# A four-layer decoder step on one core: the last k tile of a stage's first block is held back, the MLP's mean square is spread over the next blocks, and gate blocks go ahead of the first chain

## The chip, the cores and the metric

The kernel runs on one NeuronCore of a Trainium2 chip. The metric is the device time of the whole program in microseconds (us), the median of several runs. The trace comes from one profiled execution, with its own time. Engines: PE is TensorE (matmuls), DVE is VectorE, ACT is ScalarE, POOL is GpSimd, SP issues the weight transfers.

## The reference

One step of a decoder trunk of four layers for 288 tokens (256 of a prompt, 8 x 4 of samples), model width 1024. A layer is a token mixer and an MLP, each behind an RMS norm and added to x. The mixers are retention (layer 0), SSD (1), gated DeltaNet (2) and retention (3).

```
def _rms(x, w):  return x * lax.rsqrt(jnp.mean(x * x, axis=-1, keepdims=True) + 1e-6) * w
def _sqrelu_mlp(h, w_up, w_down):  return jnp.square(jax.nn.relu(h @ w_up)) @ w_down   # 1024 -> 4096 -> 1024
for i in range(4):
    out, s = (_retention, _ssd, _gdn)[i % 3](_rms(x, norm_mix[i]), ...)   # @ w_in, conv, scan, gate, norm, @ w_out
    x = x + out
    x = x + _sqrelu_mlp(_rms(x, norm_mlp[i]), mlp_w_up[i], mlp_w_down[i])
y = _rms(x, norm_final)
```

The outputs are y for prompt and samples and the new states of the mixers. SSD and gated DeltaNet (gdn) have a causal convolution over four positions and, per token, small gates: a step size or decay `la` (SSD), `g` and `beta` (gdn), from 32 columns of the input projection.

## The kernel before, in words

Tokens lie along the free axis (288 columns), channels on the 128 partitions. x is eight tiles of 128 x 288, one per k tile.

`dense` multiplies by a weight matrix, 128 output columns (a block) at a time. The weights come in as float32, 256 columns (two blocks, 1 MB) in a transfer, and are split for the matmul: ACT copies a half of a block's k tiles (four, 128 x 512) to a rounded `wh` (L212), DVE subtracts to get the rest `wl` (L215). There are four buffers for these halves: two blocks' worth. A block is 8 k tiles of three matmuls each, `xh·wh` (L227), `xl·wh` (L228), `xh·wl` (L229), where `xh` and `xl` are the activations split in the same way (`ah` and `al` in the second half of the MLP). A block gathers in a PSUM tile `psd` and is evacuated by a callback right behind its 24 matmuls.

The activations of a stage come out of the stage before, tile by tile: `norm_add(k)` scales x by the norm's gain and splits it to `xh` (ACT, L302) and `xl` (DVE, L303), and adds x's square to `acc` (DVE for the last tile, L298). The division by the root mean square is not waited for: the first matmuls run on unscaled x, and a factor `rb` is multiplied in behind. `tok_rstd` sums `acc` over the partitions on PE (`ps_st`, L330), DVE adds the constant (`ms`, L333), POOL takes the power (`rs_y`, L268); `bcast` spreads the result over the partitions on PE (`ps_bc`, L342), and ACT copies it to `rb` (L351). `norm_finish` is all of that.

With the eighth tile `norm_add` leaves a list `hold`: of the next six `wl` casts the first two (the first block) may go at once, the other four (the second and third block) are issued behind the eighth tile's `xl`.

An MLP runs `up` and `down` in four quarters q of 8 blocks each; behind the 8 blocks of `up` of q = 0 comes `norm_finish`. A mixer runs in four units m: the SSD and gdn layers start with `gates_tok` (one block of 32 columns, then `norm_finish`, then small transposes `ps_gt`), and the chain that turns the gates into decays (`ps_ct`, `cth`, `cts`). `units` runs the first projection and then weaves, for every m, the chain (scan) with gate blocks, further projections and output blocks. `conv_dense` evacuates a projection block to `U` (L815), keeps its last columns in `tl` (L818, transposed later on PE as `ps_cs`, L850) and does the convolution on DVE (L832).

What sets the order: a scheduler puts each engine's instructions in a row when the program is built, by the order in which the code emits them and by priorities; at run time every engine works through its own row, and waits where an operand isn't there.

Of the kernel before, what the change touches and what calls it, by code (L numbers as in the profile page):

```python
# [123 lines left out]
def run(gen):  # L124
    for _ in gen:
        pass


class K:
    def __init__(self, ctx, tc, I, O, C, layers):  # L130
        self.tc, self.nc, self.I, self.O, self.C = tc, tc.nc, I, O, C
        self.layers = layers
        self.hold, self.started = [], False
        self.ahead = 0
# [53 lines left out]
    def dense(self, xh, xl, w, evac, pre=None):  # L188
# [4 lines left out]
        for c0 in range(0, n, cw):  # L193
# [10 lines left out]
            for s0 in range(0, cn, sw):  # L204
# [13 lines left out]
                for o in range(0, sn, 128):  # L218
                    os = slice(o, min(o + 128, sn))
                    self.ahead -= 1  # L220
                    if 0 <= self.ahead < 2:
                        ps = self.ps("psd", "s")[:, 0:T]
                    else:
                        ps = self.psd.tile([128, T], F32, name="psd", tag="d")
                    po = ps[:os.stop - o]
                    for k in range(kt):
                        nc.tensor.matmul(po, lhsT=hs[k][:, os], rhs=xh[k], start=(k == 0), stop=False)  # L227
                        nc.tensor.matmul(po, lhsT=hs[k][:, os], rhs=xl[k], start=False, stop=False)  # L228
                        self.last_mm = nc.tensor.matmul(po, lhsT=ls[k][:, os], rhs=xh[k], start=False,  # L229
                                                        stop=(k == kt - 1))  # L230
                    evac((c0 + s0 + o) // 128, ps)
                    yield kt * 3 * 0.124

    def weave(self, chain, *fillers):
# [110 lines left out]

    def norm_finish(self):
        nc = self.nc
        r = self.tok_rstd([self.nx["acc"]], D)
# [100 lines left out]
    def mlp(self, mp, i, nxt, consts):  # L449
# [4 lines left out]
        late = self.later(mp) if self.later else iter(())  # L454
        self.later = None

        def blocks(gen):
            for _ in gen:
                next(late, None)

        for q in range(4):
            ah, al = self.act_tiles()
# [6 lines left out]
                nc.scalar.activation(ah[o], v, AF.Square)  # L469
                nc.vector.tensor_tensor(out=al[o], in0=a, in1=ah[o], op=ALU.subtract)  # L470

            blocks(self.dense(xh, xl, I["mlp_w_up"][i, :, q * 1024:(q + 1) * 1024], up))
            if q == 0:
                rb = self.norm_finish()
                rb2 = mp.tile([128, T], F32, name="rb2", bufs=1)
                nc.vector.tensor_tensor(out=rb2, in0=rb, in1=rb, op=ALU.mult)
# [30 lines left out]

        yield from self.dense(act[0], act[1], w[m * 512:(m + 1) * 512, :], ev)

    def units(self, proj, chain, gate, fin, w, i, side=None):  # L510
        acts = {}

        def finish(m):
# [3 lines left out]
        def out(n):  # L517
            yield from self.w_out(w, n, acts.pop(n), i)
# [419 lines left out]
    def ssd(self, ctx, j, i):  # L938
# [46 lines left out]
        def bcm(ap, n):  # L985
            return ap.unsqueeze(1).broadcast_to([ap.shape[0], n, ap.shape[1]])


        tok = self.gates_tok(rp, xh, xl, w[:, 6144:6176], wg, rb)
        V.tensor_tensor(out=tok, in0=tok, in1=bcm(dtb, 3), op=ALU.add)  # L990
        tok2 = tok.rearrange("p g h -> p (g h)")
# [44 lines left out]
        units = {}  # L1036

        def proj(m):
            xs = [rp.tile([128, T], F32, name="xs", tag=f"xs{a}", bufs=2) for a in range(4)]
            tails, tl = [], rp.tile([128, 8, 35], F32, name="tl", tag="tl", bufs=2)  # L1040
            Bt = [rp.tile([128, T], F32, name="Bt", tag=f"Bt{a}") for a in range(2)]
            Ct = [rp.tile([128, T], F32, name="Ct", tag=f"Ct{a}") for a in range(2)]
            for (c0, ch, dst) in ((4096 + m * 256, 16 + 2 * m, Bt), (5120 + m * 256, 24 + 2 * m, Ct),
                                  (2048 + m * 512, 4 * m, xs)):
                yield from self.conv_dense(rp, xh, xl, w[:, c0:c0 + len(dst) * 128], ch, rb, cw, cb, bias, dst, tails, tl)
            units[m] = {"xs": xs, "B": Bt, "C": Ct, "tails": tails}

        def scan(m):
            u = units[m]
# [193 lines left out]
        self.units(proj, scan, gate, fin, I["ssd_w_out"][j], i)  # L1243

# [4 lines left out]
    def gdn(self, ctx, j, i):  # L1249
# [54 lines left out]
        def small(name, *sh):  # L1304
            return rp.tile([128] + list(sh), F32, name=name)


        tok = self.gates_tok(rp, xh, xl, w[:, 6144:6176], wg, rb)
        beta, g = small("beta", 3, 16), small("g", 3, 16)
        ax = self.t128("ax")[:, 0:48].rearrange("p (g h) -> p g h", g=3)  # L1310
# [45 lines left out]
        units = {}  # L1356
# [6 lines left out]

        Z = rp.tile([128, 2, DB, 40], F32, name="Z")
        G.memset(Z, 0.0)

        def proj(m):
            qk = rp.tile([128, 4, T], F32, name="qk", tag="qk", bufs=2)
            v = [rp.tile([128, T], F32, name="v", tag=f"v{a}") for a in range(4)]
            tails, tl = [], rp.tile([128, 8, 35], F32, name="tl", tag="tl", bufs=2)  # L1370
            for (c0, dst) in ((m * 256, [qk[:, 0], qk[:, 1]]), (1024 + m * 256, [qk[:, 2], qk[:, 3]]), (2048 + m * 512, v)):
                yield from self.conv_dense(rp, xh, xl, w[:, c0:c0 + len(dst) * 128], c0 // 128, rb, cw, cb, None, dst, tails, tl)
            units[m] = {"qk": qk, "v": v, "tails": tails}

        def kt(name, tag, bufs, shape=(128, 4, 128)):
            return rp.tile(list(shape), F32, name=name, tag=tag, bufs=bufs)
# [380 lines left out]
            yield from prep(m)  # L1757
            yield from loop(m)

        self.units(proj, scan, gate, fin, I["gdn_w_out"][j], i, sample)  # L1760
        self.later = lambda pool: self.gdn_states(pool, j)

    def gdn_states(self, pool, j):
# [83 lines left out]
```

## Time and profile before

| | |
|---|---|
| median of 3 runs | 2246.93 us (2236.96 to 2248.14) |
| the profiled execution | 2250.74 us |
| its span (first to last instruction) | 2248.6 us |
| PE busy | 2172.1 us, 97%, 16348 matmuls |
| DVE, ACT, POOL busy | 1555.2 us (69%), 1242.9 us (55%), 586.0 us (26%) |
| mean granted PE clock | 0.98 of full speed |

A row of the timeline gives the start, the duration and the instruction (output<-input); in square brackets stands how long its engine sat idle ahead of it and what ended the wait. PE's matmuls overlap: their ends are modelled, so the distance between two starts, and not the duration, is the pace. [...]

### The profile page before, as it was taken

Reading aid. Unit: us, or ns where it says so; the run is one execution under the profiler, and the core shown is the slowest. Engines: PE = TensorE matmul, PEld = TensorE weight load, DVE = VectorE, ACT = ScalarE, POOL = GpSimd, SP = SyncE. Lnnn points to the kernel's source line nnn. Section 1 sums busy time; section 2 is a strip of 40 time slices with the busy share of each in tenths; the row PEclk is TensorE's granted clock in tenths of the full one; section 3 lists DMA queues with packets and bytes.
Section 4 is the critical chain, followed back from the end, with each engine's and each line's share of the span. In section 5 each row is a group of like instructions: output and inputs, shape, how many; then the busy total and the mean of one; then the engine's idle time right before and its main releaser. Section 6 shows DMA issues by size and latency. Waiting matters only on the chain. (4 is left out here: it accounts for less than half of the span.)

```text
span 2248.6 us, 43174 instructions
## 1 busy us (share of the span) xinstructions
PE 2172.1 (97%) x16348; PEld 1996.7 (89%) x16348; DVE 1555.2 (69%) x3195; ACT 1242.9 (55%) x2823; POOL 586.0 (26%) x622
## 2 busy tenths in 40 slices
PE   9999999999999999999899999999999999999998
PEld 7878899998889889999888888889899779889998
DVE  6777775557898887555786786577766677776554
ACT  4444455545687766554466676476644444445454
POOL 2100113333322322333332232134333001103333
PEclk9999999999899999999989999899999999999999
DMA  7776765545446544554443442277765666764553
GB/s 208 255 254 206 248 195 160 169 151 161 128 145 192 171 143 139 172 169 151 148 127 106 121 140 93 90 207 236 226 187 188 228 230 218 237 222 158 163 167 115
DMA packets 404219, 394.96 MB, mean 176 GB/s; under 512 B 13003, under 2 KB 353716, under 8 KB 403916
## 3 DMA queue, kind: packets, MB, share of 16 engines
q1 hardware_dynamic: 403852, 391.96, 55.0%
q8 instruction: 128, 2.10, 0.4%
q14 instruction: 79, 0.65, 0.1%
q10 hardware_dynamic: 96, 0.20, 0.0%
q0 software_dynamic: 64, 0.07, 0.0%
HBM read 333.49 MB, written 58.69 MB: 174 GB/s over the span
## 5 line engine op out<-in xcount | busy, mean ns | idle before, releaser
L212 ACT CAST wh<-raw 128x512 fp32r<-128x512 f32 x1024 | 627.8, 620 | 675.4 <-PE psd L228 629.7
L215 DVE TENSOR_TENSOR wl<-raw,wh 128x512 fp32r<-128x512 f32 x1024 | 743.3, 733 | 309.0 <-ACT wh L212 290.5
L227 PE MATMUL psd<-xh,wh 128*128 128x288 f32 x2576 | 776.4, 302 | 6.5 <-ACT xh L302 4.6
L228 PE MATMUL psd<-xl,wh 128*128 128x288 f32 x2576 | 773.4, 300 | 4.4 <-DVE xl L303 3.2
L229 PE MATMUL psd<-xh,wl 128*128 128x288 f32 x2576 | 770.3, 299 | 3.8 <-DVE wl L215 3.8
L227 PEld LDWEIGHTS psd<-xh,wh 128*128 128x128 f32 x2576 | 487.7, 190 | 27.5 <-issue 11.1
L228 PEld LDWEIGHTS psd<-xl,wh 128*128 128x128 f32 x2576 | 491.6, 191 | 18.2 <-issue 7.5
L229 PEld LDWEIGHTS psd<-xh,wl 128*128 128x128 f32 x2576 | 490.7, 191 | 11.6 <-DVE wl L215 6.7
L227 PE MATMUL psd<-ah,wh 128*128 128x288 f32 x1536 | 463.4, 302 | 5.0 <-DVE x L447 2.8
L229 PE MATMUL psd<-ah,wl 128*128 128x288 f32 x1536 | 459.8, 299 | 6.8 <-DVE wl L215 6.7
L228 PE MATMUL psd<-al,wh 128*128 128x288 f32 x1536 | 460.8, 300 | 1.6 <-issue 1.1
L227 PEld LDWEIGHTS psd<-ah,wh 128*128 128x128 f32 x1536 | 292.6, 191 | 15.3 <-ACT wh L212 5.3
L229 PEld LDWEIGHTS psd<-ah,wl 128*128 128x128 f32 x1536 | 293.9, 191 | 10.2 <-DVE wl L215 9.1
L228 PEld LDWEIGHTS psd<-al,wh 128*128 128x128 f32 x1536 | 293.3, 191 | 10.0 <-issue 7.8
L487 POOL TENSOR_TENSOR x<-x,dn 128x288 f32<-128x288 f32 x120 | 148.7, 1239 | 239.4 <-DVE dn L485 239.4
L468 POOL TENSOR_TENSOR a<-v 128x288 f32<-128x288 f32 x128 | 109.6, 857 | 270.7 <-ACT v L467 269.7
L731 DVE SCALAR_TENSOR_TENSOR S<-S,ps_up 128x512 f32<-128x512 f32 x128 | 83.4, 685 | 53.5 <-PE ps_up L730 50.8
L832 DVE SCALAR_TENSOR_TENSOR cacc<-U,cw,cacc 128x312 f32<-128x312 f32 x192 | 105.3, 554 | 13.8 <-ACT cacc L827 11.8
L470 DVE TENSOR_TENSOR al<-a,ah 128x288 fp32r<-128x288 f32 x128 | 59.9, 468 | 68.7 <-POOL a L468 67.9
L268 POOL TENSOR_TENSOR rs_y<-ms,mhalf 128x3 f32<-128x3 f32 (+3 forms) x37 | 36.2, 981 | 231.2 <-DVE ms L747 170.7
L808 POOL COPY U<-cb 128x24 f32<-128x24 f32 x64 | 34.4, 543 | 208.0 <-DVE cacc L832 140.4
L485 DVE TENSOR_TENSOR dn<-psd,rb 128x288 f32<-128x288 f32 x128 | 58.2, 455 | 40.4 <-PE psd L229 40.4
(512 smaller groups left out, 2618.5 us busy)
## 6 DMA issues: line engine op xcount, KB each, us to landing
raw<-mlp_w_up SPq DMA_DIRECT2D x64, 1024.0 KB
raw<-mlp_w_down SPq DMA_DIRECT2D x64, 1024.0 KB
raw<-ret_w_in SPq DMA_DIRECT2D x32, 1024.0 KB
S<-state_ret SPq DMA_DIRECT2D x64, 512.0 KB
s_ret<-S SPq DMA_DIRECT2D x64, 512.0 KB
raw<-ssd_w_in SPq DMA_DIRECT2D x24, 1024.0 KB
raw<-gdn_w_in SPq DMA_DIRECT2D x24, 1024.0 KB
raw<-ret_w_in SPq DMA_DIRECT2D x32, 512.0 KB
```

Of the source, the lines that this page charges most:

```text
L212: self.last_cast = nc.scalar.copy(wh, src)
L215: nc.vector.tensor_tensor(out=wl, in0=src, in1=wh, op=ALU.subtract)
L227: nc.tensor.matmul(po, lhsT=hs[k][:, os], rhs=xh[k], start=(k == 0), stop=False)
L228: nc.tensor.matmul(po, lhsT=hs[k][:, os], rhs=xl[k], start=False, stop=False)
L229: self.last_mm = nc.tensor.matmul(po, lhsT=ls[k][:, os], rhs=xh[k], start=False, stop=(k == kt - 1))
L268: self.nc.gpsimd.tensor_tensor(out=y[rows], in0=ms[rows], in1=self.mhalf[rows].broadcast_to([rows.stop - rows.start, n]), op=ALU.pow)
L468: nc.gpsimd.tensor_tensor(out=a, in0=v, in1=v, op=ALU.mult)
L470: nc.vector.tensor_tensor(out=al[o], in0=a, in1=ah[o], op=ALU.subtract)
L485: nc.vector.tensor_tensor(out=t, in0=ps, in1=rb2, op=ALU.mult)
L487: e.tensor_tensor(out=self.x[o], in0=self.x[o], in1=t, op=ALU.add)
L731: nc.vector.scalar_tensor_tensor(out=S[:, b, z], in0=S[:, b, z], scalar=C["g4"][h], in1=up, op0=ALU.mult, op1=ALU.add)
L832: nc.vector.scalar_tensor_tensor(out=acc[:, 0:n], in0=u, scalar=wk, in1=acc[:, 0:n], op0=ALU.mult, op1=ALU.add)
```

## The change

`dense` gets a counter `delay`. While it is over 0, a block's first seven k tiles are emitted, but its last k tile (three matmuls) and its evacuation are put in a list `ends`; the next block emits its own first seven, then what is in `ends`, then its own last tile. `delay` is set to 1 for each of the 8 calls of `dense` in each MLP, and for the first projection of each mixer. In the MLP `norm_finish` is cut in two: `tok_rstd` behind block 3 (counted from 0) of `up` of q = 0, and the rest (`norm_rows`: `bcast`, `rb`, and `rb2`) behind block 6. In the SSD and gdn layers the first block of the projection is emitted ahead of `gates_tok`. In `units` two gate blocks are taken ahead of the first unit's chain. No instruction is added or removed.

```diff
+                    def part(ks, po=ps[:os.stop - o], hs=hs, ls=ls, os=os):
+                        for k in ks:
+                            nc.tensor.matmul(po, lhsT=hs[k][:, os], rhs=xh[k], start=(k == 0), stop=False)
...
+                    def end(part=part, n=(c0 + s0 + o) // 128, ps=ps):
+                        part([kt - 1])
+                        evac(n, ps)
+
+                    part(range(kt - 1))
+                    if self.delay:
+                        self.delay -= 1
+                        self.ends.append(end)
+                    else:
+                        while self.ends:
+                            self.ends.pop(0)()
+                        end()
...
-        def blocks(gen):
-            for _ in gen:
+        def blocks(gen, then=()):
+            self.delay = 1
+            then = dict(then)
+            for n, _ in enumerate(gen):
                 next(late, None)
+                if n in then:
+                    then[n]()
...
+        first = ((3, lambda: rst.append(self.tok_rstd([acc0["acc"]], D))), (6, rb_done))
...
-            blocks(self.dense(xh, xl, I["mlp_w_up"][i, :, q * 1024:(q + 1) * 1024], up))
-            if q == 0:
-                rb = self.norm_finish()
...
+            blocks(self.dense(xh, xl, I["mlp_w_up"][i, :, q * 1024:(q + 1) * 1024], up), () if q else first)
...
-        run(proj(0))
+        if first is None:
+            self.delay = 1
+            first = proj(0)
+        run(first)
         for m in range(4):
             fill = [gate(m)]
+            if m == 0:
+
+                next(fill[0])
+                next(fill[0])
...
+        self.delay = 1
+        first = proj(0)
+        next(first)
         tok = self.gates_tok(rp, xh, xl, w[:, 6144:6176], wg, rb)
```

The first place is PE at the first quarter of layer 0's MLP. In the order before, the sum `ps_st` stands behind the last `up` block (`xh_3805` is the eighth tile), and four matmuls of the first `down` block (`ah`, `al`) lie between it and `ps_bc`:

```order
L229 MATMUL psd<-xh_3805,wl 128x288
L330 MATMUL ps_st<-ones,acc 128x1 x3
L227 MATMUL psd<-ah_3817,wh 128x288
L228 MATMUL psd<-al_3825,wh 128x288
L229 MATMUL psd<-ah_3817,wl 128x288
L227 MATMUL psd<-ah_3818,wh 128x288
L342 MATMUL ps_bc<-c_ident,rs_y 128x128 x2
L342 MATMUL ps_bc<-c_ident,rs_y 128x32
```

In the order of the change `ps_st` stands behind an earlier `up` block (`xh_3630` is the first tile of the next one; line numbers have moved), and three blocks, 72 matmuls, lie between it and `ps_bc`; the first of them and the last stand here:

```order
L342 MATMUL ps_st<-ones,acc 128x1 x3
L228 MATMUL psd<-xh_3630,wh 128x288
L229 MATMUL psd<-xl_3631,wh 128x288
L230 MATMUL psd<-xh_3630,wl 128x288
...
L229 MATMUL psd<-xl_3806,wh 128x288
L230 MATMUL psd<-xh_3805,wl 128x288
L354 MATMUL ps_bc<-c_ident,rs_y 128x128 x2
L354 MATMUL ps_bc<-c_ident,rs_y 128x32
```

So the sum and its spread have moved apart by 68 matmuls, both now lie inside the `up` blocks, and the same has happened in the other three MLPs.

The second place is PE at the start of the SSD layer (`xh_6499`, `xl_6500` are the eighth tile; 32x288 is the gates' block). Before, the gates' block ends, `ps_st` follows, and fifteen matmuls of the first projection block stand ahead of `ps_bc`, of which the first three and the last stand here:

```order
L229 MATMUL psd<-xh_6499,wl 32x288
L330 MATMUL ps_st<-ones,acc 128x1 x3
L227 MATMUL psd<-xh_6190,wh 128x288
L228 MATMUL psd<-xl_6191,wh 128x288
L229 MATMUL psd<-xh_6190,wl 128x288
...
L229 MATMUL psd<-xh_6365,wl 128x288
L342 MATMUL ps_bc<-c_ident,rs_y 128x128 x2
```

With the change the projection block's held tile (the three rows of 128x288 with tile 6499) stands ahead of `ps_st`, and four matmuls stand between the sum and its spread:

```order
L228 MATMUL psd<-xh_6499,wh 128x288
L229 MATMUL psd<-xl_6500,wh 128x288
L230 MATMUL psd<-xh_6499,wl 128x288
L342 MATMUL ps_st<-ones,acc 128x1 x3
L228 MATMUL psd<-xh_6499,wh 32x288
L229 MATMUL psd<-xl_6500,wh 32x288
L230 MATMUL psd<-xh_6499,wl 32x288
L228 MATMUL psd<-xh_6220,wh 128x288
L354 MATMUL ps_bc<-c_ident,rs_y 128x128 x2
```

Here sum and spread have moved together, from 15 matmuls apart to 4. In the gdn layer they go from 6 to 4, in the last layer's retention from 15 to 4.

The third place is DVE in the SSD layer's first chain, where `tl` is a projection block's last columns and `cts` the split decay. Before, the fourth block's `tl` stands behind `cts`:

```order
L818 TENSOR_TENSOR tl<-psd,rb 128x35
L215 TENSOR_TENSOR wl<-raw,wh 128x512 x2
L1034 SCALAR_TENSOR_TENSOR cts<-cth,c_sel,ps_cT 128x288
L832 SCALAR_TENSOR_TENSOR cacc<-U_6668,cw,cacc 128x312
L815 TENSOR_TENSOR U_6666<-psd,rb 128x256
L832 SCALAR_TENSOR_TENSOR cacc<-U_6668,cw,cacc 128x312
L816 TENSOR_TENSOR U_6666<-psd,rb 128x4x8
L832 SCALAR_TENSOR_TENSOR cacc<-U_6668,cw,cacc 128x312
L818 TENSOR_TENSOR tl<-psd,rb 128x35
```

With the change it stands ahead of it:

```order
L216 TENSOR_TENSOR wl<-raw,wh 128x512
L864 SCALAR_TENSOR_TENSOR cacc<-U_6600,cw,cacc 128x312
L847 TENSOR_TENSOR U_6598<-psd,rb 128x256
L864 SCALAR_TENSOR_TENSOR cacc<-U_6600,cw,cacc 128x312
L848 TENSOR_TENSOR U_6598<-psd,rb 128x4x8
L850 TENSOR_TENSOR tl<-psd,rb 128x35
L295 SCALAR_TENSOR_TENSOR xl_6828<-xr,vec,xh_6827 128x288
L1081 SCALAR_TENSOR_TENSOR cts<-cth,c_sel,ps_cT 128x288
```

So the fourth `tl`, for which PE's `ps_cs` waits, no longer stands behind an instruction that waits for PE and ACT.

## Rows read from the trace of the kernel before

**Rows 1.** The page: PE and the two cast groups (busy, mean ns).

```profile
PE 2172.1 (97%) x16348; PEld 1996.7 (89%) x16348; DVE 1555.2 (69%) x3195; ACT 1242.9 (55%) x2823; POOL 586.0 (26%) x622
...
L212 ACT CAST wh<-raw 128x512 fp32r<-128x512 f32 x1024 | 627.8, 620 | 675.4 <-PE psd L228 629.7
L215 DVE TENSOR_TENSOR wl<-raw,wh 128x512 fp32r<-128x512 f32 x1024 | 743.3, 733 | 309.0 <-ACT wh L212 290.5
```

**Rows 2.** The waits of PE: us in total, times, longest.

```profile
PE ps_bc L342 <- POOL rs_y L268: 6.5, 6, 3.0
```

**Rows 3.** The timeline of PE at the MLPs of layers 0 to 3.

```profile
350.79 0.25 PE L330 MATMUL ps_st<-ones,acc 128*128 128x1 f32 x1
...
352.62 0.60 PE L342 MATMUL ps_bc<-c_ident,rs_y 128*128 128x128 f32 x3 [0.94 <-POOL rs_y L268]
...
862.61 1.52 PE L342 MATMUL ps_bc<-c_ident,rs_y 128*128 128x128 f32 x12 [0.53 <-POOL rs_y L268]
...
1513.82 1.49 PE L342 MATMUL ps_bc<-c_ident,rs_y 128*128 128x128 f32 x6 [2.98 <-POOL rs_y L268]
...
2056.21 0.85 PE L342 MATMUL ps_bc<-c_ident,rs_y 128*128 128x128 f32 x6 [0.93 <-POOL rs_y L268]
```

**Rows 4.** Windows of half clock: length, busy (count) by engine, PEclk, DMA.

```profile
1512.80:1519.60 6.80, 5.78 (x25) 5.78 (x26) 2.33 (x5) 3.47 (x10) 1.73 (x2) 0.50 1.00 294
...
1123.70:1130.50 6.80, 6.15 (x23) 5.55 (x24) 6.80 (x16) 4.77 (x12) 4.94 (x9) 0.50 0.49 153
...
570.50:577.60 7.10, 6.52 (x28) 6.08 (x28) 5.89 (x14) 4.66 (x11) 4.36 (x4) 0.50 0.00 0
```

**Rows 5.** The timeline of ACT and POOL at layer 2's MLP.

```profile
1510.54 0.98 ACT L1805 ACTIVATE St<-St,lcd 128x128 f32<-128x128 f32 x3 [3.31 <-DMA St<-state_gdn]
...
1512.91 0.86 POOL L268 TENSOR_TENSOR rs_y<-ms,mhalf 128x3 f32<-128x3 f32 x1 [0.89 <-DVE ms L333]
```

**Rows 6.** The waits of ACT from 1490 to 1712 us.

```profile
ACT St L1805 <- DMA St<-state_gdn: 20.4, 10, 4.5
```

**Rows 7.** The timeline of PE and DVE at the start of layer 0's MLP.

```profile
326.75 0.29 PE L227 MATMUL psd<-xh,wh 128*128 128x288 f32 x1
327.64 0.40 PE L228 MATMUL psd<-xl,wh 128*128 128x288 f32 x1 [0.60 <-DVE xl L303]
...
328.27 0.36 PE L229 MATMUL psd<-xh,wl 128*128 128x288 f32 x1
...
327.07 0.51 DVE L303 SCALAR_TENSOR_TENSOR xl<-x,vec,xh 128x288 fp32r<-128x288 f32 x1
327.50 1.89 DVE L215 TENSOR_TENSOR wl<-raw,wh 128x512 fp32r<-128x512 f32 x3
```

**Rows 8.** The timeline of PE at the starts of SSD, gdn and the last mixer.

```profile
541.64 0.32 PE L227 MATMUL psd<-xh,wh 128*32 128x288 f32 x1 [1.34 <-ACT xh L302]
...
1097.97 0.32 PE L227 MATMUL psd<-xh,wh 128*32 128x288 f32 x1 [1.34 <-ACT xh L302]
...
1721.35 0.40 PE L227 MATMUL psd<-xh,wh 128*128 128x288 f32 x1 [1.40 <-ACT xh L302]
...
1725.33 0.38 PE L342 MATMUL ps_bc<-c_ident,rs_y 128*128 128x128 f32 x1 [0.19 <-POOL rs_y L268]
```

**Rows 9.** The timeline of PE and DVE at the first chain of SSD.

```profile
561.32 0.63 PE L1003 MATMUL ps_ct<-la,c_ssd_tri 128*128 128x32 f32 x4 [1.84 <-DVE la L996]
...
569.84 0.43 PE L850 MATMUL ps_cs<-c_ident,tl 128*35 128x128 f32 x1 [2.67 <-DVE tl L818]
...
567.15 0.51 DVE L1034 SCALAR_TENSOR_TENSOR cts<-cth,c_sel,ps_cT 128x288 fp32r<-128x288 f32 x1 [2.85 <-ACT cth L1033]
```

**Rows 10.** The timeline of PE at the first chain of gdn.

```profile
1114.83 0.84 PE L1302 MATMUL ps_gc<-g,gk 128*128 128x16 f32 x6 [0.29 <-DVE g L1315]
...
1120.27 0.27 PE L850 MATMUL ps_cs<-c_ident,tl 128*35 128x128 f32 x1 [0.84 <-ACT cth L833]
1124.02 0.77 PE L1302 MATMUL ps_dif<-cts,e 128*128 128x256 f32 x2 [3.48 <-DVE tl L818]
```

More of the change, by code (lines that the diff above doesn't have):

```diff
@@ L133, in __init__ @@
         self.hold, self.started = [], False
+        self.delay, self.ends = 0, []
         self.ahead = 0
@@ L224, in dense @@
                         ps = self.psd.tile([128, T], F32, name="psd", tag="d")
[L225 to L231, printed above, removed]
+                    def part(ks, po=ps[:os.stop - o], hs=hs, ls=ls, os=os):
+                        for k in ks:
+                            nc.tensor.matmul(po, lhsT=hs[k][:, os], rhs=xh[k], start=(k == 0), stop=False)
+                            nc.tensor.matmul(po, lhsT=hs[k][:, os], rhs=xl[k], start=False, stop=False)
+                            nc.tensor.matmul(po, lhsT=ls[k][:, os], rhs=xh[k], start=False, stop=(k == kt - 1))
+                    def end(part=part, n=(c0 + s0 + o) // 128, ps=ps):
[9 more added lines that the diff above has]
+                        end()
                     yield kt * 3 * 0.124
@@ L347, in norm_finish, with norm_rows @@
         nc = self.nc
-        r = self.tok_rstd([self.nx["acc"]], D)
+        return self.norm_rows(self.tok_rstd([self.nx["acc"]], D))
+    def norm_rows(self, r):
+        nc = self.nc
         ps = self.bcast(r, 0)
@@ L455, in mlp, with rb_done @@
         self.later = None
-        def blocks(gen):
-            for _ in gen:
+        def blocks(gen, then=()):
+            self.delay = 1
+            then = dict(then)
+            for n, _ in enumerate(gen):
                 next(late, None)
+                if n in then:
+                    then[n]()
+        rst = []
+        def rb_done():
+            nonlocal rb2
+            rb = self.norm_rows(rst[0])
+            rb2 = mp.tile([128, T], F32, name="rb2", bufs=1)
+            nc.vector.tensor_tensor(out=rb2, in0=rb, in1=rb, op=ALU.mult)
+        first = ((3, lambda: rst.append(self.tok_rstd([acc0["acc"]], D))), (6, rb_done))
         for q in range(4):
@@ L470, in up @@
                 nc.vector.tensor_tensor(out=al[o], in0=a, in1=ah[o], op=ALU.subtract)
-            blocks(self.dense(xh, xl, I["mlp_w_up"][i, :, q * 1024:(q + 1) * 1024], up))
-            if q == 0:
-                rb = self.norm_finish()
-                rb2 = mp.tile([128, T], F32, name="rb2", bufs=1)
-                nc.vector.tensor_tensor(out=rb2, in0=rb, in1=rb, op=ALU.mult)
+            blocks(self.dense(xh, xl, I["mlp_w_up"][i, :, q * 1024:(q + 1) * 1024], up), () if q else first)
             if q < 3 and consts:
@@ L508, in w_out, with units @@
         yield from self.dense(act[0], act[1], w[m * 512:(m + 1) * 512, :], ev)
-    def units(self, proj, chain, gate, fin, w, i, side=None):
+    def units(self, proj, chain, gate, fin, w, i, side=None, first=None):
         acts = {}
@@ L986, in bcm, with proj @@
             return ap.unsqueeze(1).broadcast_to([ap.shape[0], n, ap.shape[1]])
+        units = {}
+        def proj(m):
+            xs = [rp.tile([128, T], F32, name="xs", tag=f"xs{a}", bufs=2) for a in range(4)]
+            tails, tl = [], rp.tile([128, 8, 35], F32, name="tl", tag="tl", bufs=2)
+            Bt = [rp.tile([128, T], F32, name="Bt", tag=f"Bt{a}") for a in range(2)]
+            Ct = [rp.tile([128, T], F32, name="Ct", tag=f"Ct{a}") for a in range(2)]
+            for (c0, ch, dst) in ((4096 + m * 256, 16 + 2 * m, Bt), (5120 + m * 256, 24 + 2 * m, Ct),
+                                  (2048 + m * 512, 4 * m, xs)):
+                yield from self.conv_dense(rp, xh, xl, w[:, c0:c0 + len(dst) * 128], ch, rb, cw, cb, bias, dst, tails, tl)
+            units[m] = {"xs": xs, "B": Bt, "C": Ct, "tails": tails}
+        self.delay = 1
+        first = proj(0)
+        next(first)
         tok = self.gates_tok(rp, xh, xl, w[:, 6144:6176], wg, rb)
@@ L1034, in ssd @@
         V.scalar_tensor_tensor(out=cts, in0=cth, scalar=self.sel[:, 0:1], in1=ps[:, 0:T], op0=ALU.mult, op1=ALU.add)
[L1036 to L1046, printed above, removed]
         def scan(m):
@@ L1241, in fin @@
                     self.split(o, ah[a], al[a])
-        self.units(proj, scan, gate, fin, I["ssd_w_out"][j], i)
+        self.units(proj, scan, gate, fin, I["ssd_w_out"][j], i, None, first)
     def gdn(self, ctx, j, i):
@@ L1305, in small, with proj @@
             return rp.tile([128] + list(sh), F32, name=name)
+        units = {}
+        def proj(m):
+            qk = rp.tile([128, 4, T], F32, name="qk", tag="qk", bufs=2)
+            v = [rp.tile([128, T], F32, name="v", tag=f"v{a}") for a in range(4)]
+            tails, tl = [], rp.tile([128, 8, 35], F32, name="tl", tag="tl", bufs=2)
+            for (c0, dst) in ((m * 256, [qk[:, 0], qk[:, 1]]), (1024 + m * 256, [qk[:, 2], qk[:, 3]]), (2048 + m * 512, v)):
+                yield from self.conv_dense(rp, xh, xl, w[:, c0:c0 + len(dst) * 128], c0 // 128, rb, cw, cb, None, dst, tails, tl)
+            units[m] = {"qk": qk, "v": v, "tails": tails}
+        self.delay = 1
+        first = proj(0)
+        next(first)
         tok = self.gates_tok(rp, xh, xl, w[:, 6144:6176], wg, rb)
@@ L1354, in gdn @@
         V.scalar_tensor_tensor(out=cts, in0=cth, scalar=self.sel[:, 0:1], in1=ps[:, 0:256], op0=ALU.mult, op1=ALU.add)
-        units = {}
         Ye = rp.tile([128, 8, 128], F32, name="Ye")
@@ L1365, in gdn @@
         G.memset(Z, 0.0)
[L1367 to L1373, printed above, removed]
         def kt(name, tag, bufs, shape=(128, 4, 128)):
@@ L1758, in scan @@
             yield from loop(m)
-        self.units(proj, scan, gate, fin, I["gdn_w_out"][j], i, sample)
+        self.units(proj, scan, gate, fin, I["gdn_w_out"][j], i, sample, first)
         self.later = lambda pool: self.gdn_states(pool, j)
```

## The prediction

> **What bounds the kernel now.** I read the page first. PE is busy for 2172.1 of 2248.6 us with 16348 matmuls [rows 1], which makes 2172.1 / 16348 = 0.133 us from start to start, while DVE and ACT stand at 69% and 55%. So an order change can only win what PE loses in waits, 2248.6 - 2172.1 = 76.5 us in all, and what it loses where its clock falls to half. Then I read PE's waits, and one of them belongs to a moved instruction in every MLP: `ps_bc` waits for POOL's `rs_y` six times, 6.5 us [rows 2]. Next came the timeline at the places that the change touches, and the windows of half clock beside them; all further numbers are from there.
>
> A word on the brackets: an idle time starts at the modelled end of the last matmul, 0.29 us after its start, where the next start is due after 0.13. So a wait costs 0.16 us more than its bracket.
>
> **The MLPs' mean square.** Before, PE issues `ps_st`, four matmuls, and then stands in front of `ps_bc` while DVE and POOL finish: 0.94, 0.53, 2.98 and 0.93 us idle [rows 3]. With four times 0.16 that is 5.4 + 0.6 = 6.0 us. In the first MLP the whole way from `ps_st` to `ps_bc` takes 352.62 - 350.79 = 1.83 us [rows 3]; with the change 72 matmuls, 72 x 0.133 = 9.6 us, lie between them, so even layer 2's way, which is 3 us longer, is covered. I take all 6.0 us off. If DVE or POOL held the short instructions back by more than 9.6 us the cover would be gone, and nothing in the four rows comes near that.
>
> Layer 2 has a second item. Behind its wait the clock is at half, 0.50 from 1512.8 to 1519.6 [rows 4]: 25 matmuls take 5.78 us where 25 x 0.133 = 3.3 us would do. It comes straight behind the longest idle time of the four, and the 0.5 to 0.9 us waits have no such stretch. I take 2.5 us off, bounds 0 and 2.5.
>
> But why was layer 2's wait three times as long? ACT stood 3.31 us for a state that the DMA queues had not delivered, so that casts and DVE's `ms` were late, and POOL started `rs_y` only at 1512.91 [rows 5]. This state traffic goes on through the MLP: ACT waits 10 times, 20.4 us, for those loads [rows 6]. When PE comes 5.5 us earlier, the loads don't, and a part of the gain can be lost at a later cast. Most of ACT's waits lie under PE's work today, so I take 1.0 us as lost again, bounds 0 and 5.6 (all of 3.1 + 2.5).
>
> **The held tile inside the MLPs.** It delays the release of one half of weights: the first block's k tiles 4 to 7 come free 24 matmuls later, 3.2 us. The cast that waits for them serves the block after next. From the release PE has 3 matmuls of the running block and 12 of the next before it needs that `wh`, 15 x 0.133 = 2.0 us, and 17 before it needs `wl`, 2.3 us; the casts take 0.62 and 0.73 us [rows 1], 1.35 together. That leaves 0.9 us for hand-overs and one other instruction ahead of them. I cost it at 0. The cover is this 0.9 us; without it the price is that of the third rival.
>
> **The entries of MLPs.** Here the held tile could give `xl` of the eighth tile time. In layer 0's MLP PE waits 0.60 us for it in the first block's last tile, and `wl` casts stand in DVE's row right behind that `xl`, from 327.50 [rows 7]. These are the second block's, by `hold`. With the change PE goes on to the second block and meets its third matmul, which needs such a `wl`: 327.50 + 0.7 = 328.2. Before, the same matmul started at 328.27 [rows 7], with the first block's last three already done. Now those three come after it: 3 x 0.133 = 0.4 us lost. The last layer's MLP has the same pattern, the other two have the casts in between in both orders: + 0.8 us in all, bounds 0 and 1.
>
> **The entries of mixers.** At the entries of SSD, gdn and the last retention PE waits 1.34, 1.34 and 1.40 us for the eighth `xh` [rows 8] and somewhat more for `xl`. The held tile would step over this, but the block that comes next has its `wl` behind that `xl` too, so I let the same stall stand three matmuls into the next block: 0, with a bound of -2 for each. New is the distance between sum and spread. Four matmuls, as at the MLPs before, were worth 0.94 + 0.16 = 1.1 us of wait [rows 3]; SSD and gdn get that, and the last retention, which waits 0.19 + 0.16 = 0.35 us now [rows 8], gets 0.75.
>
> **The first chain of SSD.** `ps_ct` waits 1.84 us for `la`; PE reaches it after the same number of matmuls as before and `la` slips about as far as PE, so this stays, within 1 us. Then `ps_cs` waits 2.67 us for the fourth `tl`, because DVE sits 2.85 us in front of `cts` [rows 9]; with `tl` ahead of `cts` this goes. The clock behind it is at half: 28 matmuls take 7.1 us [rows 4], 28 x 0.133 = 3.7 us, and of the 2.8 us between (with 0.6 of waits) I take half, 1.4, since the wait for `la` that starts the trouble is still there. SSD: 1.1 - 2.67 - 1.4 = -3.0 us, bounds -6 and +2.
>
> **The first chain of gdn.** `ps_dif` waits 3.48 us for the fourth `tl`, and a `ps_cs` 0.84 us before it [rows 10]. In the new order all four `ps_cs` stand together, ahead of the two gate blocks. So I let 2.0 of these 4.3 us stay with the fourth, bounds 0 and 4.3. `g` waits for a later `rb` and for more convolution ahead of it on DVE: 1.3 us more than the 0.29 [rows 10], bounds 0 and 3. Half clock behind the chain costs 6.8 - 0.3 - 23 x 0.133 = 3.4 us [rows 4]; half of it, 1.7, goes. gdn: 1.1 - 4.3 + 2.0 + 1.3 - 1.7 = -1.6 us, bounds -7 and +5.
>
> **Sum.** -6.0 - 2.5 + 1.0 + 0.8 + 0.75 - 3.0 - 1.6 = -10.5 us (the two retention entries' gate blocks, where no chain waits: 0). The profiled execution took 2250.74 us, so it would take 2240.2. It lies 3.8 us, 0.2%, above the median of 2246.93, whose runs reach from 2236.96; I carry the difference over to the median: 2236.4 us.
>
> **What the clock rows allow.** 5.6 of the 10.5 us are clock (2.5 + 1.4 + 1.7). The rows show half clock behind waits of 2.67 to 3.48 us and none behind 0.94 [rows 3, 4, 9, 10]; between these they decide nothing, and the change leaves PE such waits at three entries. [...]
>
> **Rivals.**
>
> First: the gain is retaken. Layer 2's DMA keeps what it gave (5.6 back instead of 1.0: + 4.6), or the clock stretches only move (+ 5.6). For it: ACT's ten waits for loads. Against: they are mostly hidden from PE. Sum -4.9 to -5.9, 2241 to 2242 us; with both nearly 0. Chance 0.24.
>
> Second: it is worth more. The held tile does step over the mixers' entry waits (-2 at each of three), and the chains lose all their waits and clock (-1.4 - 1.7 - 2.0 - 1.3): down to -23, on the median about 2224 to 2232 us. For it: gates and projection blocks are different weights, and the gates' casts are small. Against: `hold` orders them all behind the same `xl`. Chance 0.15.
>
> Third, on the other side: the held tile starves the casts. It is made in 32 `dense` calls of the MLPs. If ACT or DVE has a second evacuation ahead of the late cast, the 0.9 us of slack is gone, and PE waits at each call. At 0.35 us a call that is 11 us, which eats the whole gain; from 0.7 us a call the kernel is slower, 22.4 - 10.5 = + 12 us, 2259 us. Against: ACT is busy for 55%. Chance 0.11.
>
> **Chances and range.** A change of 0.5% (11.2 us) is about what a measurement of this kernel tells from none. My forecast case, -7 to -14 us, has 0.50; its middle lies just inside that limit, so I count 0.23 of it as the same and 0.27 as faster. The first rival (0.24) is no change, the second (0.15) is faster, the third (0.11) slower. Faster 0.42, same 0.47, slower 0.11. The range for 8 in 10 leaves out the lower end of the second rival and the third: 2227 to 2249; the forecast case by itself is 2233 to 2240.
>
> **What would show it.** Right: in all four MLPs `ps_bc` has no wait behind it, layer 2's window is at full clock, `ps_st` is followed by a `ps_bc` wait of about 1 us at the three mixers' entries, and the entries of MLPs 0 and 3 wait for `wl` instead of `xl`. Wrong: PE's waits for `wl` or `wh`, a few tenths each, spread over the MLPs (third rival); PE's waits in layer 2's MLP behind ACT's state loads grow by some us (first); the waits at the mixers' entries fall under 0.5 us (second); new stretches of half clock at the SSD or gdn entry would make the forecast too low.

## The result and the profile after

The changed kernel takes 2259.93 us (median of 9 runs, 2247.56 to 2270.17) where the kernel before, in runs beside it, takes 2244.67 us (9 runs, 2236.96 to 2249.26): a ratio of 1.0066, 95% interval 1.0045 to 1.0086. It is 15 us slower, where 10.5 us faster was forecast; the measured time lies above the range of 2227 to 2249. (A ratio here takes in all runs and need not be the quotient of the two medians.)

The profiled execution of after took 2257.7 us, only 7.0 us more than the one of before (2250.74). The one of before lies 6.1 us above its median, the one of after 2.2 us below, and the last section shows a piece of 7 us in gdn that before has and after hasn't. So the two traces are compared stage by stage.

The head of the page and PE's row, after:

```profile
span 2255.9 us, 43167 instructions
## 1 busy us (share of the span) xinstructions
PE 2166.0 (96%) x16348; PEld 1989.8 (88%) x16348; DVE 1570.9 (70%) x3195; ACT 1235.6 (55%) x2823; POOL 575.8 (26%) x622
```

The work is the same, 16348 matmuls, and PE's waits have grown from 76.5 to 2255.9 - 2166.0 = 89.9 us. Its waits, after (total, times, longest):

```profile
PE psd L230 <- DVE wl L216: 17.2, 24, 2.6
PE ps_bc L354 <- POOL rs_y L280: 5.7, 7, 1.0
...
PE ps_ct L1050 <- DVE la L1043: 3.9, 1, 3.9
...
PE ps_gc L1337 <- DVE g L1363: 3.2, 1, 3.2
```

`ps_bc`'s long wait of 3.0 us [rows 2] is gone. The waits for `la` and `g`, in the first chains of SSD and gdn, have grown from 1.84 and 0.29 us [rows 9, 10]. The timeline of PE at SSD, after, answers to [rows 8, 9]:

```profile
539.52 0.32 PE L230 MATMUL psd<-xh,wl 128*32 128x288 f32 x1 [1.91 <-DVE wl L216]
543.70 1.02 PE L342 MATMUL ps_st<-ones,acc 128*128 128x1 f32 x6
546.30 0.85 PE L354 MATMUL ps_bc<-c_ident,rs_y 128*128 128x128 f32 x6 [1.03 <-POOL rs_y L280]
...
561.64 1.06 PE L1050 MATMUL ps_ct<-la,c_ssd_tri 128*128 128x32 f32 x4 [3.90 <-DVE la L1043]
...
568.33 1.07 PE L882 MATMUL ps_cs<-c_ident,tl 128*35 128x128 f32 x4
```

And DVE at the same place, after:

```profile
538.38 0.46 DVE L310 TENSOR_TENSOR acc<-acc,sq 128x288 f32<-128x288 f32 x1 [0.55 <-ACT sq L309]
...
544.76 0.16 DVE L345 TENSOR_SCALAR ms<-ps_st 128x3 f32<-128x3 f32 x1 [2.44 <-PE ps_st L342]
...
547.63 0.42 DVE L847 TENSOR_TENSOR U<-psd,rb 128x256 f32<-128x256 f32 x1 [1.19 <-ACT rb L366]
...
561.34 0.76 DVE L1043 TENSOR_TENSOR la<-sp_r,nea 128x96 f32<-128x96 f32 x4
...
568.87 0.52 DVE L1081 SCALAR_TENSOR_TENSOR cts<-cth,c_sel,ps_cT 128x288 fp32r<-128x288 f32 x1 [3.53 <-ACT cth L1080]
```

`acc` is complete at 538.84, yet PE comes to the sum at 543.70: the matmul that stands still for `wl` (539.52) is in the gates' block, and with it 19 matmuls of that block and the three of the held tile stand ahead of `ps_st`. They take 543.70 - 539.52 = 4.18 us where 22 x 0.133 = 2.9 would do, because the last twelve run at half clock (PEclk 0.50 from 541.0 to 543.7, 0.24 us from start to start). Before, the stall lay in the gates' last tile, at 541.64 [rows 8], with the sum right behind. The timeline of PE there, before:

```profile
542.49 0.72 PE L330 MATMUL ps_st<-ones,acc 128*128 128x1 f32 x6
...
546.55 0.88 PE L342 MATMUL ps_bc<-c_ident,rs_y 128*128 128x128 f32 x6
```

From the end of the stall to the sum it was 0.85 us. From the sum to its spread it was 4.06 us, for the fifteen matmuls between them ran mostly at half clock (PEclk 0.50 from 543.4 to 546.8); after it is 2.60 us. From `rb` to `la` there are 14 us, in which DVE is nearly full. The window of that stretch, before (length, then busy of PE, PEld, DVE, ACT, POOL, then PEclk, which is the granted clock as a share of full speed, DMA share, GB/s):

```profile
547.50:561.00 13.50, 11.85 (x86) 11.14 (x85) 12.78 (x41) 7.41 (x15) 1.25 (x2) 1.00 0.47 145
```

And after:

```profile
547.20:561.40 14.20, 10.54 (x76) 9.90 (x75) 12.87 (x46) 7.71 (x15) 1.76 (x3) 1.00 0.26 77
```

DVE is busy for 12.8 of 13.5 us (95%) and 12.9 of 14.2 (91%), so it has little idle time there in which a late `rb` could be made up. The timeline of PE and DVE at gdn's entry, after, answers to [rows 8, 10]:

```profile
1103.96 0.35 PE L230 MATMUL psd<-xh,wl 128*32 128x288 f32 x1 [2.32 <-DVE wl L216]
...
1108.42 0.72 PE L342 MATMUL ps_st<-ones,acc 128*128 128x1 f32 x6
1110.73 0.49 PE L354 MATMUL ps_bc<-c_ident,rs_y 128*128 128x128 f32 x2 [1.03 <-POOL rs_y L280]
...
1125.30 1.89 PE L1337 MATMUL ps_gc<-g,gk 128*128 128x16 f32 x8 [3.16 <-DVE g L1363]
1132.58 0.43 PE L882 MATMUL ps_cs<-c_ident,tl 128*35 128x128 f32 x1 [1.52 <-DVE tl L850]
...
1130.61 0.47 DVE L1402 SCALAR_TENSOR_TENSOR cts<-cth,c_sel,ps_cT 128x256 fp32r<-128x256 f32 x1
```

The windows of half clock behind these waits, after, gdn's and SSD's, answer to [rows 4]:

```profile
1124.60:1141.60 17.00, 13.86 (x51) 11.53 (x52) 14.49 (x46) 6.82 (x17) 5.66 (x9) 0.50 0.22 66
561.40:578.40 17.00, 15.46 (x56) 12.98 (x57) 13.18 (x33) 6.71 (x19) 4.79 (x6) 0.50 0.22 66
```

Neither has shortened. gdn's has gone from 6.8 to 17.0 us, and SSD's, of which [rows 4] shows the end, was this before:

```profile
563.90:577.50 13.60, 10.11 (x40) 8.46 (x39) 9.43 (x23) 7.74 (x22) 5.03 (x5) 0.50 0.27 79
```

### The profile page after: what moved, and what is told of

Its sections match the earlier page's. It is cut to its first block, busy times and chain, and to the rows that moved or that the text cites. A ratio compares the mean times of both kernels' runs of the same rounds, so it can differ in the third digit from the quotient of the medians.

```text
span 2255.9 us, 43167 instructions
## 1 busy us (share of the span) xinstructions
PE 2166.0 (96%) x16348; PEld 1989.8 (88%) x16348; DVE 1570.9 (70%) x3195; ACT 1235.6 (55%) x2823; POOL 575.8 (26%) x622
## 5 line engine op out<-in xcount | busy, mean ns | idle before, releaser
L512 POOL TENSOR_TENSOR x<-x,dn 128x288 f32<-128x288 f32 x120 | 139.7, 1170 | 237.6 <-DVE dn L510 237.6
L499 DVE TENSOR_TENSOR al<-a,ah 128x288 fp32r<-128x288 f32 x128 | 64.1, 509 | 61.4 <-POOL a L497 60.3
L333 POOL TENSOR_TENSOR acc<-acc,sq 128x288 f32<-128x288 f32 x54 | 48.5, 899 | 129.7 <-ACT sq L332 126.0
```

Of the source, the lines that this page charges most:

```text
L333: nc.gpsimd.tensor_tensor(out=acc, in0=acc, in1=sq, op=ALU.add)
L512: e.tensor_tensor(out=self.x[o], in0=self.x[o], in1=t, op=ALU.add)
```

## The experiments

All were run in several rounds beside the kernel before. First the four parts of the change, each put alone into the kernel before.

**The spread mean square.** Edit: the MLP's `first`, nothing else.

```diff
+            blocks(self.dense(xh, xl, ..., up), () if q else first)
```

> Only the MLPs' mean square is spread (sum behind block 3, spread behind block 6); everything else as before. The theory of the prediction: the four waits of ps_bc (0.94, 0.53, 2.98 and 0.93 us) go and nothing takes their place but about 1 us in layer 2, so 5 to 8 us faster than before, ratio 0.9965 to 0.998. The rival theory, that layer 2's state loads retake it: 2 to 3 us faster, with new waits of PE for the state update in layer 2's MLP. If the whole change's 15 us loss lay in the MLPs, this one or the next would be slower by many us.

Measured: 2240.13 against 2243.85 us, ratio 0.9984 (0.9971 to 0.9997). About 3.6 us faster: between the two theories, nearer to the rival. PE's waits in layer 2's MLP in this run:

```profile
PE psd L228 <- ACT ah L497: 2.4, 1, 2.4
PE ps_st L342 <- DVE St L1840: 1.5, 1, 1.5
PE psd L228 <- ACT xh L314: 1.4, 1, 1.4
```

`ps_bc` isn't among them; the sum itself now waits for the state update, and a later matmul for `ah`.

**The held tile in the MLPs.** Edit: `blocks` alone.

```diff
         def blocks(gen, then=()):
+            self.delay = 1
```

> Only the held last k tile in the 32 dense calls of the MLPs. Theory 1 (the loss lies at the mixers' entries and first chains): within 2 us of before, + 0.8 us for the entries of the first and the last MLP. Rival (the held tile starves the casts inside the MLPs): 10 us or more slower, with waits for wl and wh at many of the 32 calls.

Measured: ratio 1.0008 (0.9995 to 1.0022), 2245.02 us. PE's waits for `wl` are 12.0 us in 17 waits, against 10.5 us in 16 before, so no call is starved; theory 1 holds.

**Two gate blocks ahead.** Edit:

```diff
             fill = [gate(m)]
+            if m == 0:
+                next(fill[0])
+                next(fill[0])
```

> Only two gate blocks ahead of the first unit's chain, in every mixer. Theory 1a (the loss comes of the entry order: projection block ahead of the gates, sum and spread 4 matmuls apart): this is neutral or faster by up to 4 us, because the waits for tl (2.7 us in SSD, 3.5 us in gdn) go. Theory 1b (the loss comes of the two gate blocks, whose evacuations and normalised inputs load DVE in front of the chain): slower by 6 to 12 us.

Measured: ratio 1.0010 (0.9996 to 1.0024), 2245.62 us. That is 1.8 us slower in the medians, and by the interval between 1 us faster and 5 us slower: theory 1b is out, theory 1a's neutral end is not.

**The mixers' entries.** Edit in SSD and gdn (the two retention layers keep the held tile alone):

```diff
+        self.delay = 1
+        first = proj(0)
+        next(first)
         tok = self.gates_tok(rp, xh, xl, w[:, 6144:6176], wg, rb)
```

> Only the mixers' entries: in SSD and gdn the projection's first block ahead of the gates' block, and its last k tile held (in the retention layers the held tile alone). Theory 1a: slower by 8 to 15 us: ps_bc waits 1 us in each of three mixers, rb comes later, so la in SSD and g in gdn come 2 to 3 us later and PE waits for them, and stretches of half clock follow. Theory 1b: within 3 us of before.

Measured: ratio 1.0047 (1.0024 to 1.0069), 2258.23 us. Theory 1a: this part makes up most of the loss. (The quotient of the medians is 1.0064.) The four ratios add up to 0.9984 + 1.0008 + 1.0010 + 1.0047 - 3 = 1.0049, against 1.0066 for the whole (1.0045 to 1.0086). The timeline of PE, then DVE, at SSD in this run:

```profile
546.31 0.85 PE L354 MATMUL ps_bc<-c_ident,rs_y 128*128 128x128 f32 x6 [1.03 <-POOL rs_y L280]
...
561.64 0.64 PE L1039 MATMUL ps_ct<-la,c_ssd_tri 128*128 128x32 f32 x2 [3.90 <-DVE la L1032]
...
561.33 0.76 DVE L1032 TENSOR_TENSOR la<-sp_r,nea 128x96 f32<-128x96 f32 x4
...
568.86 0.52 DVE L1070 SCALAR_TENSOR_TENSOR cts<-cth,c_sel,ps_cT 128x288 fp32r<-128x288 f32 x1 [3.53 <-ACT cth L1069]
```

The waits are those of after, 1.03, 3.90 and 3.53 us, without the gate blocks and without the MLPs' parts.

The trace shows only the cheaper of two groups of executions. Three of the eight take 2245.5 to 2250.3 us at a granted clock of 0.982 to 0.985, the profiled one among them; five take 2258.2 to 2260.0 us at 0.978 or 0.979. Of the kernel before, 3 of the 31 executions beside it have 0.979 or less. The middle of the three is 5.6 us above the kernel before's median; the rest of the loss goes with the lower granted clock of the five, and no trace shows where they spend it.

Why the entry costs so much was the next question: is it that `rb` is late, or that the projection's convolution stands ahead of the gates' work on DVE?

**The entry, with the sum early.** Edit, in SSD and gdn (and `rb()` calls `norm_rows(st["st"])`):

```diff
         next(first)
+        st["st"] = self.tok_rstd([self.nx["acc"]], D)
         tok = self.gates_tok(...)
```

> The entry order alone, as in the run before (+ 10 to 14 us), but the sum ps_st stands right behind the projection block's seven k tiles, ahead of the gates' block, in SSD and gdn. Theory L (the loss is that rb comes late, 3.4 us in SSD and 4.5 us in gdn, and DVE, which has no slack between rb and the end of the first chain, is late by that): rb comes about 3 us earlier than in the entry order, and 6 to 9 us come back; ratio to before 0.999 to 1.003. Rival D (the loss is the projection block's convolution, which stands in DVE's row ahead of the gates' work): rb is earlier and the loss stays, ratio 1.004 to 1.006.

Measured: ratio 1.0021 (1.0003 to 1.0038), 2252.59 us. About half of the loss comes back, though the two intervals overlap. In SSD `rb` was 2.1 us earlier in the stage and its end 2.9 us (table below); in gdn the 24 matmuls between the early sum and its spread ran at half clock, 0.24 us from start to start, and `rb` was no earlier. PE, SSD:

```profile
538.39 0.83 PE L342 MATMUL ps_st<-ones,acc 128*128 128x1 f32 x6 [1.54 <-DVE acc L310]
...
559.53 0.63 PE L1040 MATMUL ps_ct<-la,c_ssd_tri 128*128 128x32 f32 x4 [3.90 <-DVE la L1033]
```

**The gates' block first, but held.** Edit: as before, and in `gates_tok` and behind it

```diff
+        self.delay = 1
         run(self.dense(xh, xl, w, ev, wg))
...
         tok = self.gates_tok(...)
+        next(first)
```

> The gates' block stays first, as before, but it is the gates' block whose last k tile is held behind the projection's first block, in SSD and gdn; nothing else is changed. The sum ps_st follows 21 matmuls later than before, and 4 matmuls ahead of its spread. Theory L: rb is 2.5 to 3.5 us late, so 5 to 9 us slower, ratio 1.002 to 1.004. Rival D: the gates' work stands first on DVE as before, so within 2 us of before.

Measured: ratio 1.0020 (1.0001 to 1.0038), 2251.23 us. The gates' work is first on DVE and it is slower all the same: theory L, against rival D. It doesn't show a late `rb` alone, for the gates' block itself ends later too.

**The same with the sum early.** Edit: `st["st"] = self.tok_rstd(...)` between the two lines above.

> As the run with the gates' block held, but the sum ps_st stands right behind the gates' first seven k tiles, and its spread behind the projection's first block. Theory L: rb comes 0.5 to 1 us earlier than before, so 0 to 3 us faster than before, and 5 to 10 us faster than with the late sum. Rival D: the same time as with the late sum.

Measured: ratio 1.0009 (0.9991 to 1.0028), 2249.89 us. Not faster than before, and no more than 2 to 3 us better than with the late sum: short of what theory L said.

**The whole change with the sum early.**

> The whole change, with the sum ps_st moved ahead of the gates' block in SSD and gdn. Theory L: 6 to 10 us of the change's 15 us come back, 2249 to 2254 us. With rival D or with a loss in other parts: 2256 to 2262 us as the whole change.

Measured: ratio 1.0050 (1.0033 to 1.0068), 2255.79 us. 0.16%, 3.6 us, come back; neither expectation holds cleanly.

**DVE spared.** Edit: most of `softplus` left out, in the kernel before and in the entry order; what is left computes a rough decay.

```diff
-        V.reciprocal(a, a)
...
-        for k in (15, 13, 11, 9, 7, 5, 3):
-            V.scalar_tensor_tensor(out=p, in0=p, scalar=1.0 / k, in1=s2, op0=ALU.add, op1=ALU.mult)
...
+        V.tensor_tensor(out=r, in0=u, in1=r, op=ALU.add)
```

> The kernel before with most of the softplus left out (13 short DVE operations a layer, 3.7 us in SSD and about 2.7 in gdn, all between rb and the first chain; the decays are then only rough). Theory L: 3 to 6 us faster than before, since PE's wait for la goes and the decays come earlier. Rival (DVE isn't the bound there): within 1 us of before.

> The entry order alone with the same part of the softplus left out. Theory L: what DVE is spared covers the late rb in part; 2 to 6 us slower than the kernel before with the short softplus, and 8 us or more faster than the entry order with the whole. Rival (the loss is PE's own waits and clock at the entry): still 8 to 14 us slower than the kernel before with the short softplus.

Measured: 0.9994 (0.9984 to 1.0004) for the kernel before, 1.0000 (0.9988 to 1.0013) for the entry order. So by these ratios the entry's price falls from 0.47% to 0.06% when DVE has 3.7 us less to do between `rb` and the chain. That speaks against the rival that PE's own waits at the entry are the loss, for those waits are still there. But the kernel before gains about 1 us, in an interval that takes in no change, where 3 to 6 were expected: that is what its own rival said. The timeline of PE, then DVE, at SSD in the entry order with the short softplus:

```profile
546.08 0.85 PE L354 MATMUL ps_bc<-c_ident,rs_y 128*128 128x128 f32 x6 [1.03 <-POOL rs_y L280]
554.55 0.53 PE L1030 MATMUL ps_ct<-la,c_ssd_tri 128*128 128x32 f32 x4
...
553.96 0.77 DVE L1023 TENSOR_TENSOR la<-sp_r,nea 128x96 f32<-128x96 f32 x4
559.28 0.52 DVE L1061 SCALAR_TENSOR_TENSOR cts<-cth,c_sel,ps_cT 128x288 fp32r<-128x288 f32 x1 [1.86 <-ACT cth L1060]
```

The wait of 1.03 us for the sum is the same, PE's wait for `la` is gone, `la` and `cts` come 7.4 and 9.6 us earlier.

The two traces say less than the ratios. By the table below the entry order with the short softplus still puts SSD's end back by 4.4 us and gdn's by 3.2, against 5.6 and 5.8 with the whole (0.7 us of gdn's columns left out, as said there). The ratios gain beside that from the clock: neither of these two kernels has an execution with a granted clock under 0.982. So it is shown that PE's wait for `la` is made on DVE, and that the dear executions go with it; that DVE passes on the whole delay isn't shown.

**The sum first.** The attempt at a version better than both: the spread mean square, and `rb()` under a high priority, so that PE takes the sum among the gates' own matmuls and DVE takes `ms` ahead of the held casts.

```diff
+                with self.tc.high_priority(HP):
                     st["rb"] = self.norm_finish()
```

> The MLPs' spread mean square alone (1 to 6 us faster than before) and, in SSD and gdn, the sum chain of the entry ahead of everything that can wait: ps_st among the gates' own matmuls, ms ahead of the held wl casts on DVE, ps_bc ahead of the gates' last k tile. Theory L (DVE has no slack from rb to the end of the first chain, so the stage moves with rb): rb comes about 3 us earlier in SSD and 1 to 2 us earlier in gdn, for a wait of PE of about 1 us each; 3 to 5 us faster than with the spread mean square alone, ratio to before 0.996 to 0.9975. Rival (the loss was PE's own waits and clock at the entry): PE waits for the sum in both places, so 1 to 3 us slower than with the mean square alone.

Measured: ratio 0.9985 (0.9971 to 0.9999), 2239.46 us: the same as the spread mean square alone. An earlier `rb` gives nothing here, against theory L. PE, SSD:

```profile
538.21 0.83 PE L342 MATMUL ps_st<-ones,acc 128*128 128x1 f32 x6 [2.24 <-DVE acc L310]
540.60 1.49 PE L354 MATMUL ps_bc<-c_ident,rs_y 128*128 128x128 f32 x6 [0.76 <-POOL rs_y L280]
...
557.31 0.63 PE L1043 MATMUL ps_ct<-la,c_ssd_tri 128*128 128x32 f32 x4 [0.19 <-DVE la L1036]
...
565.98 0.43 PE L876 MATMUL ps_cs<-c_ident,tl 128*35 128x128 f32 x1 [3.59 <-DVE tl L844]
```

The wait for `la` has shrunk to 0.19 us, and `ps_cs` waits 3.59 us for `tl` instead.

**The spread mean square without layer 2.**

```diff
+            blocks(..., () if q or i == 2 else first)
```

> The MLPs' spread mean square in layers 0, 1 and 3 alone; layer 2's MLP, the one that also loads and stores the gdn states, as before. Theory R (layer 2's share is retaken by PE's and ACT's waits for the state traffic): the same time as with all four, about 3 us faster than before, ratio 0.9975 to 0.9995 and within 0.0008 of the run with all four (0.9984). Rival (each MLP gives its wait): layer 2's share of 3 to 5 us is missing, ratio 0.9995 to 1.0005.

Measured: ratio 0.9989 (0.9975 to 1.0004), 2244.12 us. It lies where theory R put it, 0.0005 from the run with all four, but the interval takes in the rival too.

The traces in one table, worked out by subtraction: microseconds from the start of a fixed projection matmul ahead of the stage (the 3000th `psd` for SSD, the 6144th for gdn) to `rb`, `cts` and a fixed one behind it (the 4128th, the 7104th).

```
                              SSD: rb    cts    end       gdn: rb    cts    end
kernel before                   21.1   40.7   239.9         13.6   29.4   224.9
spread mean square              21.0   40.8   240.2         13.6   32.0   226.3
held tile in MLPs               19.7   40.7   239.7         13.4   32.2   226.6
gate blocks                     21.0   40.2   242.0         13.9   32.3   229.1
sum first                       19.3   39.5   241.2         13.4   32.6   226.4
gates held, sum early           20.1   40.7   243.0         15.0   30.7   226.9
gates held                      22.4   43.5   243.6         17.3   33.3   230.4
entry, sum early                22.3   43.5   242.6         18.4   38.4   232.2
entry                           24.4   46.1   245.5         18.1   37.0   231.4
whole change, sum early         22.0   43.1   245.0         16.6   36.2   229.6
whole change                    24.1   45.8   247.7         18.1   37.1   233.0
before, short softplus          21.0   31.6   237.2         14.7   24.7   224.3
entry, short softplus           24.4   36.7   241.6         18.3   29.0   228.2
```

In SSD the entry order makes `cts` 46.1 - 40.7 = 5.4 us later and the end 245.5 - 239.9 = 5.6. But the end doesn't follow `cts` alone. With the gates held and the sum early it is 3.1 us late with `cts` in its old place, and the entry with the short softplus ends 1.7 us later than the kernel before although its `cts` comes 4.0 us earlier. In gdn the usual end is about 226.4, with `cts` at about 32; the kernel before, as profiled, lies below that. The five gdn rows with the entry or the gates held, but without the whole change, have sixteen short `ps_qs` matmuls ahead of their end that stand behind it in the other rows; 0.7 us of these ends is that. The gate blocks put the ends back by 1.6 to 2.7 us in five of six pairs (in gdn against the usual 226.4) without making `cts` later.

## Why the prediction was wrong, point by point

**The first chains: the step that failed.** The prediction put the SSD's entry and chain at -3.0 us and gdn's at -1.6; by the table they are + 7.8 and + 8.1 (+ 6.7 against the spread mean square alone, whose `cts` is the usual one). The words that failed are "`la` slips about as far as PE, so this stays". Counted from the fixed matmul ahead of SSD (at 526.41 before, 523.12 after), PE came to `ps_ct` 1.5 us later and `la` 3.6 us later, so PE stood there for 3.90 us instead of 1.84; in gdn it stood for `g` 3.16 us instead of 0.29, where 1.3 us more was forecast.

Behind that, `rb` came 3.0 us late in SSD and 4.5 in gdn. The prediction counted only the wait between sum and spread (forecast 1.1, measured 1.03 + 0.16). What it left out is the way from the stall to the sum: the stall moved from the last tile of the gates' block to the first tile of a second block, so 22 matmuls came between, and SSD's way grew from 0.85 to 4.18 us, gdn's from 1.12 to 4.46. The stall itself ended 1.2 us (SSD) and 1.8 us (gdn) later. Against this, SSD's way from the sum to the spread became 1.5 us shorter: 1.2 + 3.3 - 1.5 = 3.0. DVE, which was read at 69% over the kernel, is at 91 to 95% from `rb` to `la` and made none of it up.

How much of the loss is the late `rb` is shown in part only. With the sum early 2.9 of SSD's 5.6 us come back in the entry order, and 2.7 of 7.8 in the whole change. The rest stays open: holding the gates' block with the sum early costs SSD 3.1 us with `rb` 1.0 us earlier than before, and an earlier `rb` in the run with the sum first gives nothing. Which DVE operations behind `cts` set the end isn't settled either, nor what part of the lower clock in five of the entry's eight executions is the order's doing.

**The wait of `ps_cs` for `tl`** did go in SSD, 2.67 us, as forecast; 2.06 us came back in front of `ps_ct`. In gdn 1.52 us of waiting for `tl` stayed, where 2.0 were forecast.

**The clock behind the chains** (1.4 + 1.7 us): wrong sign. That a wait starts the half clock behind it was the author's estimate; the traces show only that the one follows the other. The longer waits for `la` and `g` are followed by 17.0 us of half clock each, against 13.6 and 6.8 before. The rows that the prediction weighed left out the stretches of 3.4 us at half clock from 543.4 and 1099.8, behind the 1.34 us waits at the entries [rows 8]; after, such a stretch lies on the 22 matmuls ahead of the sum (PEclk 0.50 from 541.0 to 543.7 in SSD).

**The MLPs' mean square.** Mechanism right, size off: 8.5 - 1.0 = 7.5 us were forecast, 3.6 measured. Layer 0's MLP gives 1.2 us (1600th to 1920th `psd`: 45.06 us before, 43.86 with the spread) and layer 3's 1.2 (10800th to 11130th: 47.33 and 46.11); layer 1's 0.7 doesn't stand out from the scatter. Layer 2's 3.1 + 2.5 - 1.0 didn't come. From the 7664th to the 9216th `psd`, the end of gdn and layer 2's MLP, ten executions without the spread take 231.8 to 236.8 us, 234.2 in the mean, and four with it 232.5 to 237.0, 234.4. That fits the DMA half of the first rival, within a scatter of some 2 us. After, the sum and the state matmul wait for the state update:

```profile
1504.43 0.83 PE L342 MATMUL ps_st<-ones,acc 128*128 128x1 f32 x6 [1.98 <-DVE St L1850]
...
1612.34 1.77 PE L1826 MATMUL ps_x<-lkv,u 64*128 64x256 f32 x4 [2.02 <-DVE St L1850]
```

The rival's clock half shows here too: layer 2's half clock at 1512.8 [rows 4] is gone, and after has 6.8 us of it from 1612.7, behind the second of these waits.

**The entries of MLPs** went as forecast: a `wl` wait of 1.07 and 1.06 us in place of 0.60 [rows 7] and, in layer 3, 0.58 for `xl`, at the second block's third matmul. After, layers 0 and 3:

```profile
327.25 0.40 PE L230 MATMUL psd<-xh,wl 128*128 128x288 f32 x1 [1.07 <-DVE wl L216]
...
2040.42 0.40 PE L230 MATMUL psd<-xh,wl 128*128 128x288 f32 x1 [1.06 <-DVE wl L216]
```

**The mixers' entry stall** stood where it was forecast, in the next block's third matmul, but it was put at no change and grew: 1.91 us at 539.52 and 2.32 at 1103.96, where PE waited 1.34 + 0.25 and 1.34 + 0.51 for `xh` and `xl`. **The held tile inside the MLPs** cost nothing that the runs can tell (ratio 1.0008, 0.9995 to 1.0022), as forecast: the third rival is out.

**The rivals and bounds** missed the case that came. The third rival's 2259 us lies next to the 2259.93 measured by luck: its cause, starved casts in the MLPs, isn't there. The upper bounds for the two chains, + 2 and + 5 us, were passed by 6 and by 2 to 3. What the prediction lacked is the count of matmuls between the stall and the sum, and an engine that is nearly full in one stretch and at 69% overall.

## What to carry to other kernels

Before work is put into a stall, count what comes to stand between the stall's end and the instruction that everything waits for: here 22 matmuls, 4.2 us, ahead of the sum. Ask what each moved instruction's result feeds, and read the busy share of that engine in the stretch behind it, not over the kernel. A wait that hangs on a transfer can be worth little when another engine waits for the same transfers: here 4.6 us on paper, nothing that stands out of a scatter of 2 us in ten executions against four. And one profiled execution can be the cheap one of its kernel, as the entry order's was (2250.3 us at a granted clock of 0.983, where five of eight took 2258.2 us or more at 0.978 or 0.979): compare its granted clock with that of the other runs.

## What was not expected of the hardware

One stretch of half clock comes and goes between executions. In gdn's tail, from the 7488th to the 7680th `psd`, the kernel before takes 61.2 us with this window in it (before):

```profile
1430.90:1448.00 17.10, 17.10 (x110) 14.30 (x110) 2.89 (x6) 5.31 (x13) 0.00 (x0) 0.50 0.01 1
```

The run with the gates' block held has it too and takes 61.4 us. After takes 54.5 us there, the spread mean square alone 53.9 and the entry order 54.7, all without it. Six of fourteen profiled executions have it, of kernels with the change's parts and without. The run without layer 2 has it (61.3 us) and the spread mean square hasn't, though DVE, ACT and POOL work through the same rows in both up to 1490 us. That is 7 us, two thirds of what was forecast; the clock terms of the prediction were read from one execution too. No run here shows what sets off a stretch that comes and goes like this, some 7 us each time.
